# A decoder trunk on one core: other accumulator banks for a second weight tile, output stores on another queue, and accumulating loads pinned behind accumulating splits

## The chip, the core and the metric

The kernel runs on one core of a Trainium2 chip. A core has a matmul engine (TensorE, PE in the profile; its weight loads are listed apart as PEld), a vector engine (VectorE, DVE), a scalar engine (ScalarE, ACT), a general engine (GpSimd, POOL) and a synchronisation engine (SyncE, SP) that here only issues transfers. Each engine runs its own instructions in order. Transfers are issued by SyncE, ScalarE and GpSimd; the page lists their queues as q1 (SyncE's), q10 (ScalarE's) and q0 (GpSimd's). Sums of matmuls are kept in PSUM, which has eight banks here, each for 128 x 512 numbers of four bytes.

The metric is the device time of one execution in microseconds (us): a median over several runs, beside one execution that the hardware profiler recorded.

## The reference

Two layers, each of three residual blocks on x of 512 tokens by 1024 channels in float32, and a final norm:

```
for l in range(DEPTH):                                   # DEPTH = 2
    x = x + 0.5 * swiglu(rms_norm(x, ffn1_norm[l]), ffn1_wg[l], ffn1_wu[l], ffn1_wd[l])
    z = rms_norm(x, mix_norm[l]) @ w_in[l]
    attn_out = sliding_window_attention(q, k, v, attn_sink[l])   # q, k, v cut from z
    conv_out = short_conv(...)                                   # the rest of z
    x = x + concatenate([attn_out, conv_out]) @ w_out[l]
    x = x + 0.5 * swiglu(rms_norm(x, ffn2_norm[l]), ffn2_wg[l], ffn2_wu[l], ffn2_wd[l])
return rms_norm(x, final_norm)
swiglu(h, w_gate, w_up, w_down) = (silu(h @ w_gate) * (h @ w_up)) @ w_down   # 1024 -> 2816 -> 1024
```

## The kernel before

**Number format.** Every float32 operand is split into a high part "hi" of a shorter format and the rest "lo", and a product takes three matmuls: hi*hi, hi*lo and lo*hi. For weights, `split` (line 197) is a ScalarE cast (hi) and a VectorE subtraction (lo). `split_far` (line 201) spares VectorE: ScalarE writes lo = -raw, rounded to the short format (line 203), and casts hi (line 204), and then GpSimd issues a transfer that adds raw to lo (line 205); which leaves raw - hi there; the transfer waits for ScalarE.

**Weights.** A unit is one weight tile of 512 KB in one of eight "raw" buffers. `need_raw` (line 184) traces the loads up to a given unit: SyncE loads the first block of the unit (`load`, line 182), and when a unit is a sum of two blocks, GpSimd issues a second part, a transfer that adds the second block to the first (line 193). `need_split` (line 207) asks for raw units some way ahead and splits the next ones in the order of the plan; `take_split` hands the split tile to the matmuls, with splitting two tiles ahead of use.

**Stages of an FFN.** `FIRST`, `INNER` and `LAST` (lines 32 to 40) list the stages: "p" computes 256 hidden channels plainly, "w" computes 512 by a seven-product scheme (Winograd's form of Strassen) with forms a11, a12, s2, s3, s1, a22, s4, each in two halves of its contraction, "d" is the down-projection of plainly computed channels, "s" a down-projection by the seven-product scheme. INNER and LAST begin ("p", 0), ("d", (0,)), ("w", 1). In these, the weight tiles of ("d", (0,)), two of them, and form a11, half 0, of ("w", 1) are split far. The units of ("w", 1) are, in twos for the halves: a11 (one block), s1 (two blocks), a12 (one), s3 (two), a22 (one). The FFNs with INNER or LAST are the second of layer 0 and both of layer 1, so this stretch is run three times.

**Accumulators.** The eight banks have three names (`psum`, line 92): four "mm", two "sc", two "aux". `down` (line 306) goes over the eight 128-channel blocks of x. For ("d", (0,)) a weight tile covers four blocks, and the first tile is computed by `level` (lines 292 to 304), which takes its four blocks abreast in four "mm" banks; the second tile is computed by `group` (lines 265 to 286), block after block, in "mm" banks too. Behind each block VectorE adds the sum to x (line 992), and thereby frees the bank. Stage w (`winograd2`, line 863) keeps its sums "x" in "mm", "y" in "sc" and "w" in "aux". The norm's sum of squares (`factors`) uses one "aux" bank for a moment in stage p.

**Order.** The kernel's framework lays out each engine's instructions from their dependences and from the order in which the program traces them. Only the first group of the kernel and the last token tiles are ordered by hand (`manual_schedule`, for ScalarE and VectorE at the end). `tc.issue_after(ins)` makes every instruction that its block traces on the engine of `ins` follow `ins` in that engine's order, without a wait for its completion.

**The end.** `Finale.down` (line 1092) computes the last down-projection with tokens on the partitions, token tile by token tile (`piece`), and closes each tile by the norm's factor (`factor`, or `guess` and `mend`), a scaling of its two halves (`scale`, line 1111: half 0 by ScalarE at line 1118, half 1 by VectorE at line 1114), and a store of each half (line 1120): half 0 from ScalarE's queue, half 1 from SyncE's.

Of the kernel before, what the change touches and what calls it, by code (L numbers as in the profile page):

```python
# [15 lines left out]
P = 128  # L16
# [42 lines left out]
def trunk_kernel(  # L59
# [32 lines left out]
    def psum(tag, shape, name):  # L92
        return ps.tile(shape, F32, tag=tag, bufs={"mm": 4, "sc": 2, "aux": 2}[tag], name=name)
# [21 lines left out]
    def f32(ap):  # L115
        return ap.bitcast(F32)
# [67 lines left out]
    def need_raw(u):  # L184

        while state["raw"] <= min(u, len(units) - 1):
            n = state["raw"]
            _, _, kc, _, wide = units[n][0]
            r = stock(f"raw_{n}", shape=(P, kc, wide))
            if n:  # L190
                load(r, n, 0, kc)
            for more in units[n][1:]:
                nc.gpsimd.dma_start(out=r, in_=rows_of(*more), accum_op=ALU.add)  # L193
            raw_of[n] = r
            state["raw"] += 1
# [5 lines left out]
    def split_far(hi, lo, raw):  # L201

        nc.scalar.activation(lo, raw, AF.Copy, scale=-1.0)
        nc.scalar.copy(hi, raw)
        nc.gpsimd.dma_start(out=f32(lo), in_=raw, accum_op=ALU.add)

    def need_split(g):
        while state["split"] <= min(g, len(order) - 1):
            n = state["split"]
            u, what = order[n]  # L210
            far = what == "far"
            if what in (None, "wide", "far"):
                need_raw(u if far else u + LOAD_AHEAD)
                raw = raw_of.pop(u)
            elif isinstance(what, tuple):

                what, h, how = what
                far = how == "far"
                last = {"a11": 0, "a12": 4, "s2": 2, "s3": 6, "s1": 2, "a22": 8, "s4": 4}[what]
                need_raw(u + max(last, 4) + h + (0 if far else LOAD_AHEAD))  # L220
                a11, s1, a12, s3, a22 = (raw_of.get(u + 2 * i + h) for i in range(5))
                if what == "s2":
                    late = state["late"] if h else None
                    with tc.issue_after(late) if late else nullcontext():
                        nc.vector.tensor_add(a11, a11, s1)  # L225
                raw = {"a11": a11, "a12": a12, "s2": a11, "s3": s3, "s1": s1, "a22": a22, "s4": a12}[what]
            else:

                need_raw(u + 4 + LOAD_AHEAD)
                a11, a12, s1, s3, a22 = (raw_of.get(u + i) for i in range(5))  # L230
                if what == "s2":
                    nc.vector.tensor_add(a11, a11, s1)
                if what == "s4":
                    nc.vector.tensor_add(a11, a11, a12)
                raw = {"a11": a11, "a12": a12, "s2": a11, "s3": s3, "s1": s1, "a22": a22, "s4": a11}[what]
                if what == FORMS[-1]:
                    for i in range(5):
                        del raw_of[u + i]
            shape = list(raw.shape)
            hi = wpool.tile(shape, F32R, tag="wh", bufs=3, name=f"wh_{n}")  # L240
            lo = wpool.tile(shape, F32R, tag="wl", bufs=3, name=f"wl_{n}")
            if far:
                split_far(hi, lo, raw)
            elif n:
                split(hi, lo, raw)
            if isinstance(order[n][1], tuple):
                if what == "s3" and how == "share":
                    nc.gpsimd.dma_start(out=a12, in_=a11, accum_op=ALU.add)
                elif what == "s3":
                    nc.vector.tensor_add(a12, a12, a11)  # L250
                done = {"s3": (0, 3), "s1": (1,), "a22": (4,), "s4": (2,)}.get(what, ())
                for i in done:
                    del raw_of[u + 2 * i + h]
            split_of[n] = (hi, lo)
            state["split"] += 1
            if far:
                need_raw(u + LOAD_AHEAD + (4 + h if isinstance(order[n][1], tuple) else 0))

    def take_split(ahead=SPLIT_AHEAD):
        n = state["group"]  # L260
# [1 line left out]
        need_split(n + ahead if n else 0)  # L262
        return n, *split_of.pop(n)

    def group(rhs, between=None, own=None, order=range(KC)):

        n, hi, lo = own or take_split()
        acc = psum("mm", [P, S], f"acc_{n}")
        order = order[: len(rhs)]
        first, last = order[0], order[-1]  # L270
        late = n in (1, 2, 3)
        for k in order:
            if between:
                between(k, hi, lo)
            nc.tensor.matmul(acc, hi[:, k, :], rhs[k][0], start=k == first, stop=False)  # L275
            if n == 0:
                nc.tensor.matmul(acc, lo[:, k, :], rhs[k][0], start=False, stop=False)
            nc.tensor.matmul(  # L278
                acc, hi[:, k, :], rhs[k][1], start=False, stop=n == 0 and k == last
            )  # L280
            if n != 0 and not late:
                nc.tensor.matmul(acc, lo[:, k, :], rhs[k][0], start=False, stop=k == last)  # L282
        if late:
            for k in order:
                nc.tensor.matmul(acc, lo[:, k, :], rhs[k][0], start=False, stop=k == last)
        return acc
# [19 lines left out]
    def down(rhs, fresh=False):  # L306

        wide = abreast(len(rhs))
        for c in range(0, KC, wide):
            n, hi, lo = take_split()  # L310
            if fresh and c == 0:
                yield from enumerate(level(n, hi, lo, rhs, wide))
                continue
            for j in range(wide):
                cols = slice(j * P, (j + 1) * P)
                yield c + j, group(rhs, own=(f"{n}_{j}", hi[:, :, cols], lo[:, :, cols]))

    def plan():
        def cols(src, k0, kc, n, how=None):
# [683 lines left out]
    class Finale:  # L1003
# [88 lines left out]
        def down(self, rhs):  # L1092
            for half in range(2):
                gb = g2(f"gain_{half}")
                nc.sync.dma_start(
                    gb, final_norm[half * S : (half + 1) * S].partition_broadcast(P)
                )
                self.gain.append(gb)
            done = small("done", NT)
            self.widen(0, len(rhs) // 2)  # L1100
            for t in range(NT):
                rest = done[:, t : t + 1]
                acc = self.products(rhs, 0, t, 0, S)
                self.close(acc, 0, t, 0, rest)
                nc.vector.tensor_scalar(rest, rest, 1.0 / D, EPS, op0=ALU.mult, op1=ALU.add)
                if t == 0:
                    self.widen(1, len(rhs) // 2)
            def factor(t, ssq):
                return self.root(t, ssq, done[:, t : t + 1])

            def scale(t, by, h):
                y = self.y[t][h]
                if h:
                    nc.vector.scalar_tensor_tensor(
                        y, y, by, self.gain[h], op0=ALU.mult, op1=ALU.mult
                    )
                else:
                    nc.scalar.activation(y, y, AF.Copy, scale=by)
                cols = slice(h * S, (h + 1) * S)
                (nc.sync if h else nc.scalar).dma_start(out[0, t * P : (t + 1) * P, cols], y)  # L1120

            def piece(t, c0, wide):
                ssq = small(f"ssq_end{t}_{c0}", 1)
                self.close(self.products(rhs, 1, t, c0, wide), 1, t, c0, ssq)
                return ssq

            for t in range(NT - 2):
                by = factor(t, piece(t, 0, S))
                for h in (1, 0):
                    scale(t, by, h)  # L1130


            a, b = NT - 2, NT - 1
            with tc.manual_schedule(engines={act, dve}):
                ssq = piece(a, 0, S)
                early = self.guess(a, ssq, done[:, a : a + 1])
                first = piece(b, 0, H)
                by = self.mend(a, ssq, done[:, a : a + 1], early)
                scale(a, by, 0)
                second = piece(b, H, H)  # L1140
                scale(a, by, 1)
                rest = done[:, b : b + 1]
                nc.vector.scalar_tensor_tensor(
                    rest, first, 1.0 / D, rest, op0=ALU.mult, op1=ALU.add
                )
                by = self.mend(b, second, rest, self.guess(b, second, rest))
                for h in (1, 0):
                    scale(b, by, h)
# [252 lines left out]
```

## Time and profile before

| what | value |
|---|---|
| median of 3 runs | 1687.75 us (1687.32 to 1688.72) |
| the profiled execution | 1686.98 us, of which 1685.2 us are its span |
| granted clock of TensorE, mean | 0.999 |
| PE busy, share of the span | 1674.2 us, 99% |
| PEld, DVE, ACT, POOL busy | 86%, 82%, 57%, 12% |
| moved by transfers | 283.14 MB, mean 168 GB/s |

The span goes from the first to the last instruction in the profile. A row of the timeline has the start and the duration in us, the engine, the line of the program, the operation, what is written and read, and in brackets how long the engine had been idle and which instruction's end released it. Rows with a "q" behind the engine's name belong to its sequencer, which issues transfers. A row of a window has the window, its length, then busy time and number of instructions for PE, PEld, DVE, ACT and POOL, the granted clock, the busy share of the sixteen transfer engines and GB/s. A row of the list of waits has who waited for whom, the total in us, how many times, and the longest. A row of transfers has their number, their size, and the median time from issue to landing.

### The profile page before, as it was taken

How to read it: one execution, taken by the hardware profiler on the slowest of the kernel's cores; microseconds unless marked ns; L12 is line 12 of the kernel's file. 1: busy time of each engine (PE TensorE's matmuls, PEld its weight loads, DVE VectorE, ACT ScalarE, POOL GpSimd, SP SyncE). 2: the span in 40 equal slices, each digit the busy share in tenths (PEclk: the TensorE clock that was granted, in tenths of full speed). 3: DMA queues.
4: the chain of work that ended last, by engine and by line, in shares of the span. 5: the costliest groups of instructions: out<-in, count | busy, mean ns of one | idle time of the engine just before them, and what ended most of it. 6: DMA issues, size and time to landing. Idle time of an engine off the chain costs nothing.

```text
span 1685.2 us, 23535 instructions
## 1 busy us (share of the span) xinstructions
PE 1674.2 (99%) x9014; PEld 1444.2 (86%) x9014; DVE 1380.9 (82%) x1817; ACT 965.5 (57%) x1333; POOL 207.6 (12%) x186
## 2 busy tenths in 40 slices
PE   9999999999999999999999999999999999999998
PEld 7888889988898888889988888999888988888886
DVE  7987679988899967799798677997788997667995
ACT  6545565466566655564465555654565766555654
POOL 1011111001111111111011111110012111111111
PEclk9999999999999999999999999999999999999999
DMA  8467777731497677778567777875125867777881
GB/s 251 101 174 189 187 199 184 186 95 51 120 231 172 166 187 187 187 189 222 154 142 183 179 185 186 200 192 170 51 63 139 224 138 200 183 181 186 225 212 51
DMA packets 191558, 283.14 MB, mean 168 GB/s; under 512 B 8972, under 2 KB 77652, under 8 KB 191444
## 3 DMA queue, kind: packets, MB, share of 16 engines
q1 hardware_dynamic: 151108, 199.95, 37.5%
q0 software_dynamic: 39184, 80.23, 28.3%
q8 instruction: 71, 1.16, 0.3%
q10 hardware_dynamic: 1152, 1.45, 0.2%
q14 instruction: 43, 0.35, 0.1%
HBM read 261.14 MB, written 2.10 MB: 156 GB/s over the span
## 4 chain that ended last, share of the span: by engine, by line
PE 96%; DVE 3%; issue 0%; ACT 0%; ACTq 0%; DVEq 0%
PE x L713 25%; PE y L713 12%; PE x_s L698 8%; PE acc L275 8%; PE acc L278 8%; PE acc L282 7%; PE w L713 6%; PE y_s L698 4%; PE x_s L713 3%; PE w_s L698 2%; PE at L919 2%; PE x_m L698 1%; PE y_m L698 1%; PE y_s L713 1%; PE pt L1248 1%; PE x L833 1%
## 5 line engine op out<-in xcount | busy, mean ns | idle before, releaser
L198 ACT CAST wh<-raw 128x1024 fp32r<-128x1024 f32 (+1 forms) x484 | 507.3, 1048 | 545.7 <-PE x L713 131.4
L199 DVE TENSOR_TENSOR wl<-raw,wh 128x1024 fp32r<-128x1024 f32 (+1 forms) x483 | 588.9, 1221 | 209.0 <-ACT wh L198 207.4
L275 PE MATMUL acc<-xh,wh 128*128 128x512 f32 x448 | 176.4, 394 | 0.2 <-ACT xh L422 0.2
L278 PE MATMUL acc<-xl,wh 128*128 128x512 f32 x448 | 175.3, 391 | 0.1
L282 PE MATMUL acc<-xh,wl 128*128 128x512 f32 x416 | 162.3, 390 | 0.0
L193 POOL DMA_DIRECT2D raw<-in_ffn_wu_dram x39 | 47.2, 1210 | 531.6 <-DMA raw<-in_ffn_wu_dram 327.4
L278 PEld LDWEIGHTS acc<-xl,wh 128*128 128x128 f32 x448 | 84.2, 188 | 18.8 <-DVE xl L423 1.6
L275 PEld LDWEIGHTS acc<-xh,wh 128*128 128x128 f32 x448 | 84.3, 188 | 17.4 <-ACT xh L422 0.6
L282 PEld LDWEIGHTS acc<-xh,wl 128*128 128x128 f32 x416 | 78.1, 188 | 16.2
L193 POOL DMA_DIRECT2D raw<-in_ffn_wg_dram x39 | 47.2, 1233 | 228.6 <-DVE wl L199 89.6
L225 DVE TENSOR_TENSOR raw<-raw,raw 128x1024 f32<-128x1024 f32 x58 | 70.4, 1219 | 1.0 <-DMA raw<-in_ffn_wu_dram 0.4
L193 POOL DMA_DIRECT2D raw<-in_ffn_wd_dram x32 | 38.6, 1214 | 257.2 <-DMA raw<-in_ffn_wd_dram 111.5
L713 PE MATMUL w<-wh,fb21h 128*128 128x512 f32 x152 | 60.7, 399 | 0.0
L713 PE MATMUL x<-wh,ft2h 128*128 128x512 f32 x152 | 60.6, 398 | 0.0
L713 PE MATMUL y<-wh,ft3h 128*128 128x512 f32 x152 | 60.4, 398 | 0.0
L713 PE MATMUL w<-wl,fb21h 128*128 128x512 f32 x152 | 59.4, 391 | 0.0
L713 PE MATMUL x<-wl,ft2h 128*128 128x512 f32 x152 | 59.3, 390 | 0.0
L713 PE MATMUL y<-wh,ft3l 128*128 128x512 f32 x152 | 59.2, 390 | 0.0
L713 PE MATMUL y<-wl,ft3h 128*128 128x512 f32 x152 | 59.2, 390 | 0.0
L713 PE MATMUL w<-wh,fb21l 128*128 128x512 f32 x152 | 59.2, 389 | 0.0
L713 PE MATMUL x<-wl,fb11h 128*128 128x512 f32 x152 | 59.2, 389 | 0.0
L713 PE MATMUL x<-wh,fb11h 128*128 128x512 f32 x152 | 59.1, 389 | 0.0
(502 smaller groups left out, 4789.6 us busy)
## 6 DMA issues: line engine op xcount, KB each, us to landing
raw<-in_ffn_wu_dram SPq DMA_DIRECT2D x127, 512.0 KB, 3.8
raw<-in_ffn_wd_dram SPq DMA_DIRECT2D x104, 512.0 KB, 5.1
raw<-in_ffn_wg_dram SPq DMA_DIRECT2D x87, 512.0 KB, 4.8
raw<-in_ffn_wu_dram POOLq DMA_DIRECT2D x39, 512.0 KB, 8.1
raw<-in_ffn_wg_dram POOLq DMA_DIRECT2D x39, 512.0 KB, 6.0
raw<-in_w_in_dram SPq DMA_DIRECT2D x36, 512.0 KB, 3.7
raw<-in_ffn_wd_dram POOLq DMA_DIRECT2D x32, 512.0 KB, 8.0
raw<-raw POOLq DMA_DIRECT2D x20, 512.0 KB, 7.2
```

The source lines that it names most:

```text
L193: nc.gpsimd.dma_start(out=r, in_=rows_of(*more), accum_op=ALU.add)
L198: nc.scalar.copy(hi, raw)
L199: eng.tensor_sub(lo, raw, f32(hi))
L225: nc.vector.tensor_add(a11, a11, s1)
L275: nc.tensor.matmul(acc, hi[:, k, :], rhs[k][0], start=k == first, stop=False)
L278: nc.tensor.matmul(acc, hi[:, k, :], rhs[k][1], start=False, stop=n == 0 and k == last)
L282: nc.tensor.matmul(acc, lo[:, k, :], rhs[k][0], start=False, stop=k == last)
L698: nc.tensor.matmul(accs[c // 2][:, c % 2, :], w[:, k, cols], x_[:, 2 * h + k, :], start=start and c % 2 == 0 and h + k + i == 0, stop=h + ...
L713: nc.tensor.matmul(accs[u], x_[:, 2 * h + k, tok], w[:, k, :], start=start and h + k + i == 0, stop=h + k == 2 and i == 2, skip_group_chec ...
L833: nc.tensor.matmul(out, w[:, k, cols], x_[:, k, :], start=start and k + i == 0, stop=k == KC // 2 - 1 and i == 2, skip_group_check=not start,)
L919: nc.tensor.transpose(tp[:, t * P : (t + 1) * P], ups[t][:, c * P : (c + 1) * P], ident)
L1248: nc.tensor.transpose(tp[:, h, :], self.p[:, h, kb * P : (kb + 1) * P], ident)
```

## The change

Three things are changed, and nothing that is computed.

- `group` gets the name of its bank as an argument, and `down` gives the second weight tile of ("d", (0,)) the names sc, sc, aux, aux for its four blocks instead of mm.
- `split_far` returns its transfer, and the `need_raw` that follows a far split is traced under `tc.issue_after` of that transfer. Its engine is GpSimd, so this concerns the second parts (line 193). For a form that is split far, the `need_raw` ahead of the split asks only for the form's own unit; the rest is asked for behind it.
- The stores of half 0 are issued by SyncE instead of ScalarE, but for the last token tile's, which stays with ScalarE.

```diff
@@ -202,7 +202,7 @@
         nc.scalar.activation(lo, raw, AF.Copy, scale=-1.0)
         nc.scalar.copy(hi, raw)
-        nc.gpsimd.dma_start(out=f32(lo), in_=raw, accum_op=ALU.add)
+        return nc.gpsimd.dma_start(out=f32(lo), in_=raw, accum_op=ALU.add)
@@ -217,7 +217,7 @@
                 last = {"a11": 0, "a12": 4, "s2": 2, "s3": 6, "s1": 2, "a22": 8, "s4": 4}[what]
-                need_raw(u + max(last, 4) + h + (0 if far else LOAD_AHEAD))
+                need_raw(u + h if far else u + max(last, 4) + h + LOAD_AHEAD)
@@ -240,7 +240,7 @@
             if far:
-                split_far(hi, lo, raw)
+                sent = split_far(hi, lo, raw)
@@ -254,7 +254,9 @@
             if far:
-                need_raw(u + LOAD_AHEAD + (4 + h if isinstance(order[n][1], tuple) else 0))
+
+                with tc.issue_after(sent.ins):
+                    need_raw(u + LOAD_AHEAD + (4 + h if isinstance(order[n][1], tuple) else 0))
@@ -262,10 +264,10 @@
-    def group(rhs, between=None, own=None, order=range(KC)):
+    def group(rhs, between=None, own=None, order=range(KC), tag="mm"):
         n, hi, lo = own or take_split()
-        acc = psum("mm", [P, S], f"acc_{n}")
+        acc = psum(tag, [P, S], f"acc_{n}")
@@ -313,7 +315,9 @@
             for j in range(wide):
                 cols = slice(j * P, (j + 1) * P)
-                yield c + j, group(rhs, own=(f"{n}_{j}", hi[:, :, cols], lo[:, :, cols]))
+                own = (f"{n}_{j}", hi[:, :, cols], lo[:, :, cols])
+                tag = ("sc", "sc", "aux", "aux")[j] if fresh else "mm"
+                yield c + j, group(rhs, own=own, tag=tag)
@@ -1117,7 +1121,8 @@
                 cols = slice(h * S, (h + 1) * S)
-                (nc.sync if h else nc.scalar).dma_start(out[0, t * P : (t + 1) * P, cols], y)
+                queue = nc.scalar if h == 0 and t == NT - 1 else nc.sync
+                queue.dma_start(out[0, t * P : (t + 1) * P, cols], y)
```

## The prediction

> **What bounds the kernel now.** I read the page's head first, then a window over the closing stage, then the list of who waited for whom on the matmul engine.
>
> ```profile
> span 1685.2 us, 23535 instructions
> PE 1674.2 (99%) x9014; PEld 1444.2 (86%) x9014; DVE 1380.9 (82%) x1817; ACT 965.5 (57%) x1333; POOL 207.6 (12%) x186
> ```
>
> ```profile
> 1670.00:1685.20 15.20, 8.21 (x48) 7.11 (x46) 7.91 (x26) 8.22 (x19) 0.09 (x1) 0.90 0.37 141
> ```
>
> ```profile
> PE acc L275 <- DVE x L992: 1.9, 3, 0.7
> ...
> PE y_m L698 <- DVE wl L199: 0.5, 2, 0.2
> ```
>
> PE is busy 1674.2 of 1685.2 us, so 11.0 us are idle. 15.20 - 8.21 = 7.0 of them lie in the closing window, and of the other 4.0 the largest item is one kind of wait, three times, 1.9 us in all: the matmul of line 275, which writes an accumulator, waits for VectorE's eviction of line 992. Nothing in the change can be worth much more than those three waits and a part of the closing 7.0 us, unless it makes PE wait where it doesn't wait now. The three places lie in the FFNs whose stage list is not FIRST:
>
> ```profile
> 537.09 1.07 PE L301 MATMUL acc<-a,wh 128*128 128x512 f32 x4
> 538.84 0.50 PE L275 MATMUL acc<-a,wh 128*128 128x512 f32 x1 [0.68 <-DVE x L992]
> 539.40 0.40 PE L282 MATMUL acc<-a,wl 128*128 128x512 f32 x1
> ...
> 874.75 0.50 PE L275 MATMUL acc<-a,wh 128*128 128x512 f32 x1 [0.56 <-DVE x L992]
> ...
> 1371.14 0.50 PE L275 MATMUL acc<-a,wh 128*128 128x512 f32 x1 [0.68 <-DVE x L992]
> ```
>
> ```profile
> 536.96 1.23 DVE L534 TENSOR_TENSOR sums<-sums,hf 128x1024 f32<-128x1024 f32 x1
> 538.10 1.28 DVE L992 SCALAR_TENSOR_TENSOR x<-acc,x 128x512 f32<-128x512 f32 x2
> ...
> 544.50 1.88 DVE L992 SCALAR_TENSOR_TENSOR x<-acc,x 128x512 f32<-128x512 f32 x3
> ```
>
> Line 301 ends the first weight tile, whose four sums fill all four "mm" banks. Line 275 begins the second tile and needs one of them back, and VectorE comes to the first eviction only behind an operand sum (L534).
>
> **The banks.** The second tile now writes two "sc" and two "aux" banks. Nothing else uses them there: the last user of "aux" is the norm's sum of squares in the stage before, and "sc" has had none since the block before. Four matmuls of line 301 take 1.07 us and the last of them 0.39, as the row of line 282 has a usual one, so they start (1.07 - 0.39) / 3 = 0.227 us apart. A matmul that waits for nothing thus starts 0.39 - 0.227 = 0.16 us ahead of its forerunner's end, where line 275 starts 0.68 behind it: 0.84 us lost, and 0.50 - 0.39 = 0.11 more because the first matmul after the wait lasts longer, in all 0.95. The second place has 0.56 + 0.16 + 0.11 = 0.83, the third 0.95 again. Sum: 2.73 us. The other bound of this term is what the list of waits has, 1.9.
>
> Where does the lateness go? VectorE's evictions are as late as before, but the next to want banks are the two "x" sums of stage w, and these get the "mm" banks that the evictions of 538.10 free, five microseconds ahead. "aux" is wanted next by that stage's "w" sums, "sc" later still by its "y" sums (with the Finale, by transposes that wait for all eight evictions in any case).
>
> ```profile
> 550.01 5.44 PE w L713 x24
> ```
>
> The last evictions end at 544.50 + 1.88 = 546.4, and "w" will start at 550.01 - 0.95 = 549.1, so 2.7 us of cover remain. Cost: none; without that cover PE would wait for "aux" as it now does for "mm".
>
> **The second parts on POOL's queue.** This part moves work. A far split is two copies on ScalarE and an accumulating transfer that POOL issues (L205). The second part of a load whose unit is a sum of two blocks is an accumulating transfer from POOL too (L193). Before:
>
> ```profile
> 514.57 2.45 POOL L193 DMA_DIRECT2D raw<-in_ffn_wu_dram  x2 [26.68 <-DVE xl L448]
> 524.00 0.90 POOL L205 DMA_DIRECT2D wl<-raw  x1 [6.98 <-ACT wl L203]
> 529.43 0.86 POOL L205 DMA_DIRECT2D wl<-raw  x1 [4.53 <-ACT wl L203]
> 532.62 1.21 POOL L193 DMA_DIRECT2D raw<-in_ffn_wg_dram  x1 [2.32 <-DMA raw<-in_ffn_wu_dram]
> 534.12 0.90 POOL L205 DMA_DIRECT2D wl<-raw  x1 [0.29 <-DVE a L199]
> ...
> 859.97 0.90 POOL L205 DMA_DIRECT2D wl<-raw  x1 [8.51 <-ACT wl L203]
> ...
> 1356.31 0.90 POOL L205 DMA_DIRECT2D wl<-raw  x1 [6.54 <-ACT wl L203]
> ```
>
> ```profile
> 544.86 0.39 PE L713 MATMUL x<-wl,fb11h 128*128 128x512 f32 x1
> ...
> 880.78 0.39 PE L713 MATMUL x<-wl,fb11h 128*128 128x512 f32 x1
> ...
> 1377.18 0.39 PE L713 MATMUL x<-wl,fb11h 128*128 128x512 f32 x1
> ```
>
> ```profile
> 549.70 1.22 DVE L225 TENSOR_TENSOR raw<-raw,raw 128x1024 f32<-128x1024 f32 x1
> ```
>
> The order is: the two second parts of form s1 (514.57), the far transfers of down tiles 1 and 2 (524.00, 529.43), the second part of s3, half 0 (532.62), the far transfer of a11, half 0 (534.12). The pins make it: tile 1, s1 half 0, tile 2, s1 half 1, a11, then s3. So the s1 parts leave some 10 and 14 us later; they now queue behind a POOL instruction that waits for ScalarE, and who waits for them is VectorE's sum at 549.70. The a11 transfer no longer stands behind s3's part. But tile 2's and a11's transfers now each follow an s1 part closely, and a11's "wl" is read first at 544.86, 880.78 and 1377.18, which the bank part brings forward to 543.9, 879.95 and 1376.2.
>
> What does one more transfer in that line cost? From issue to landing, in windows around single rows of POOL (tile 1 at the first and the second place; the two s1 parts; s3's part; a11):
>
> ```profile
> wl<-raw POOLq DMA_DIRECT2D x1, 512.0 KB, 4.5
> ```
>
> ```profile
> wl<-raw POOLq DMA_DIRECT2D x1, 512.0 KB, 5.8
> ```
>
> ```profile
> raw<-in_ffn_wu_dram POOLq DMA_DIRECT2D x1, 512.0 KB, 5.9
> ...
> raw<-in_ffn_wu_dram POOLq DMA_DIRECT2D x1, 512.0 KB, 9.8
> ```
>
> ```profile
> raw<-in_ffn_wg_dram POOLq DMA_DIRECT2D x1, 512.0 KB, 6.0
> ...
> wl<-raw POOLq DMA_DIRECT2D x1, 512.0 KB, 7.8
> ```
>
> The two s1 parts are issued half of 2.45 us apart, so they land 9.8 + 1.2 - 5.9 = 5.1 us apart. s3's part lands at 532.62 + 6.0 = 538.6 and a11's transfer at 534.12 + 7.8 = 541.9, 3.3 us apart. A place in the line thus costs 3.3 to 5.1 us, and I take 3.3, because that pair is of the same two kinds at the same point of the stage. Tile 1 lands at 524.00 + 4.5 = 528.5, and four transfers back to back behind it bring a11 to 528.5 + 13.2 = 541.7, 2.2 us ahead of 543.9. At the second place it is 859.97 + 5.8 + 13.2 = 879.0, 1.0 ahead of 879.95; at the third (with the first's 4.5, an estimate) 1356.31 + 4.5 + 13.2 = 1374.0, 2.2 ahead of 1376.2. Tile 2 lands at 528.5 + 6.6 = 535.1, ahead of the 538.0 at which PE now wants it; the second s1 part at 538.4, well ahead of 549.70; s3's parts at 545.0 and 548.3, and their splits come behind that sum. Cost at 3.3: none. At 5.1 a11 lands at 548.9, 5.0 us late.
>
> ```profile
> q0 software_dynamic: 279, 0.57, 102.9%
> q1 hardware_dynamic: 1, 0.00, 0.2%
> ```
>
> These rows are the queues in the window 872.6 to 876. A load of SyncE's (q1) had been issued at its start, and it moved 1 packet while POOL's transfers (q0) moved 279, so I don't expect SyncE's loads to stretch POOL's line there. Here the Trainium skill speaks against the change: in "DMA: Bandwidth & Descriptors", section "Queues, rings and completion order", each DMA engine goes round-robin between the queues that have work, packet by packet. By that rule a SyncE load would share with POOL's line and stretch it toward the upper bound, the case of the first rival; this window doesn't agree with it.
>
> The a11 split now asks for no unit beyond its own before it, which puts one plain SyncE load (a12, half 0) behind it in the program. SyncE's loads keep their order among themselves, and a12 is read only by the third take of the stage, behind both halves of a11; cost none, or if it is late the same wait as a late a11.
>
> **The stores.** The closing 7.0 us hold this chain:
>
> ```profile
> 1677.92 0.72 ACT L1118 ACTIVATE ytok<-ytok,y_end 128x512 f32<-128x512 f32 x1
> 1678.67 0.34 ACTq L1120 DMA_DIRECT2D out_dram<-ytok  x1
> 1679.06 0.42 ACT L1073 ACTIVATE ysq<-ytok 128x256 f32<-128x256 f32 x1 [0.42 <-DVE ytok L1071]
> ```
>
> ```profile
> 1678.24 0.42 DVE L1071 SCALAR_TENSOR_TENSOR ytok<-end,ytok 128x256 f32<-128x256 f32 x1 [0.42 <-PE end L1064]
> ```
>
> ScalarE's last square (1679.06) has its input at 1678.24 + 0.42 = 1678.66, but the issue of token tile 2's store, 0.34 us, stands between it and the scaling. That store goes to SyncE, so the square starts at about 1678.71, and the last norm factor, scaling and stores come 0.35 us earlier. The two earlier issues on ScalarE lie ahead of waits for VectorE and are worth nothing. SyncE gets three more issues of about 0.35 us, the last ready at 1677.92 + 0.72 = 1678.64, ahead of the final stores, which stay on two queues. Bounds: 0, if SyncE's longer line delays the final store, and 1679.06 - 1678.67 = 0.39. I take 0.35, from the input's row.
>
> **Sum.** 2.73 + 0.35 = 3.08 us. The profiled execution took 1686.98 us, 1.78 us of it outside its span, and would come to 1683.90. It is 0.77 us below the median of the runs shown, 1687.75; against that median the sum gives 1684.67.
>
> **Rivals.**
>
> One, slower: a11's far transfer is late. If a place in POOL's line costs y us, PE loses 4y - 15.4, 4y - 14.2 and 4y - 15.4 at the three places, each where it is positive. The first loss comes at y = 3.55, the gain of 3.08 is used up at y = 4.0, the kernel is slower by 3.4 us at y = 4.3, and at 5.1 the places lose 5.0 + 6.2 + 5.0 = 16.2: 1684.7 + 16.2 = 1700.9. Halfway into it, at y = 4.4, they lose 2.2 + 3.4 + 2.2 = 7.8: 1692.5. For it: 5.1 stands in the trace, a stage earlier. Against: 3.3 is the row for these very transfers, and the line has holes, since tile 2's and a11's transfers wait for ScalarE.
>
> Two, the wait is not removed but moves: the instructions are laid out anew around the other banks, and PE waits for an eviction or a split a little later in the same stage. Then only the stores' 0.35 is left, 1687.4. For it: VectorE is busy nearly all the time there (L534, then L992, without a gap). Against: every bank asked for next is free microseconds ahead.
>
> Three, more comes free than I count: a new layout also removes the y_m waits (0.5 us), 1684.2. Nothing in the change touches them.
>
> **How the numbers follow.** A difference under 0.2%, 3.4 us, is about what a measurement of this kernel can't tell from none, so the line on the fast side is 1684.4. The forecast falls 0.3 us short of it, and its case is split. Forecast, with 1684.0 to 1685.7 as its own range: 0.62, of which 0.18 beyond the line. Rival one: 0.15, of which 0.10 slower by over 3.4 us. Rival two: 0.17. Rival three: 0.06, of which 0.04 beyond the line and, for a layout that turns out worse instead, 0.02 slower. Faster 0.22, within 0.66, slower 0.12. The range runs from 1683.7, rival three less the 0.4 by which the fastest run lies under the median, to 1688.6, rival two with the slowest run's 1.0 and a rival one of up to y = 4.08; about 0.15 is left out, nearly all above.
>
> **What would show it.** Right: PE waits for DVE x L992 nowhere and the first matmul of line 275's second tile lasts 0.39; POOL's rows from 524 to 536 read L205, L193, L205, L193, L205; ScalarE's last square starts 0.05 us behind VectorE's last L1071. Wrong: a wait of PE at x L713 for the DMA wl<-raw (rival one), a wait of PE for DVE x L992 at L713 or L919 (rival two), or a final store of SyncE's that starts behind ScalarE's.

## The result, and the profile after

The changed kernel takes 1683.89 us, median of 10 runs (1683.20 to 1685.67), against 1687.72 (10 runs, 1687.11 to 1691.79) of the kernel before beside it. The ratio is 0.9975, with a 95% interval of 0.9966 to 0.9985: 3.83 us or a quarter of a per cent faster. That is inside the predicted range and 0.8 us below the predicted 1684.7, but beyond the bound of 0.2%, so "within 0.2%", the likeliest outcome of the prediction, did not come true.

The profiled execution of the changed kernel took 1685.67 us, the slowest of its ten. Its head, and all rows of the list of PE's waits (who waited for whom, total us, times, longest):

```profile
span 1683.8 us, 23539 instructions
PE 1674.7 (99%) x9014; PEld 1445.5 (86%) x9014; DVE 1380.8 (82%) x1817; ACT 965.4 (57%) x1333; POOL 207.5 (12%) x186
```

```profile
PE idle L125 <- DVE warm L584: 1.2, 1, 1.2
PE xt L602 <- DMA xin<-in_x_dram: 0.7, 1, 0.7
PE y_m L702 <- DVE wl L199: 0.5, 2, 0.3
```

The three waits for VectorE's eviction are gone. The execution was slow in its opening. Matched matmul by matmul with the kernel before, it runs 1.70 us behind from there on. The second row, a late load of x, is the smaller part: the first matmul behind it is 0.57 us late. The rest arises between 7.4 and 10.5 us, where matmuls last 0.59 to 0.78 us that last 0.39 to 0.50 in the kernel before; why isn't known, and the windows' rows have a granted clock of 1.00 there. No part of the change touches the opening: just ahead of the first of the three places the banks alone and the kernel with one pin (below), which wait as long for x, lie 0.7 and 0.3 us ahead of the kernel before, and the one with the earlier update 0.2 us behind. The 1.70 has to be taken out before the traces are compared.

The three places in the timeline of PE, the last matmuls of the first weight tile and the first of the second:

```profile
538.84 1.07 PE L303 MATMUL acc<-a,wh 128*128 128x512 f32 x4
539.74 0.39 PE L277 MATMUL acc<-a,wh 128*128 128x512 f32 x1
539.97 0.39 PE L280 MATMUL acc<-a,wh 128*128 128x512 f32 x1
...
874.86 0.39 PE L277 MATMUL acc<-a,wh 128*128 128x512 f32 x1
...
1370.33 0.39 PE L277 MATMUL acc<-a,wh 128*128 128x512 f32 x1
```

Line 277 (275 before) starts 538.84 + 1.07 - 539.74 = 0.17 us ahead of the end of its forerunner and lasts 0.39, where it started 0.68 behind it and lasted 0.50. The first readers of form a11's lo tile, a few microseconds on, tell what that is worth:

```profile
545.64 0.39 PE L717 MATMUL x<-wl,fb11h 128*128 128x512 f32 x1
...
880.75 0.39 PE L717 MATMUL x<-wl,fb11h 128*128 128x512 f32 x1
...
1376.22 0.39 PE L717 MATMUL x<-wl,fb11h 128*128 128x512 f32 x1
```

Against 544.86, 880.78 and 1377.18 before, these are 0.78 late, 0.03 early and 0.96 early. From the 1.70 of the opening the three places thus gain 1.70 - 0.78 = 0.92, then 0.81, then 0.93: 2.66 us. Counted from just ahead of each place to its reader they gain 0.97, 0.86 and 0.99; a few hundredths are lost again between the places.

POOL's timeline at the first place (a row with L205 is a far transfer, one with L193 a second part):

```profile
525.75 0.86 POOL L205 DMA_DIRECT2D wl<-raw  x1 [36.17 <-ACT wl L203]
526.30 1.54 POOL L193 DMA_DIRECT2D raw<-in_ffn_wu_dram  x1
531.19 0.90 POOL L205 DMA_DIRECT2D wl<-raw  x1 [3.35 <-ACT wl L203]
531.75 1.58 POOL L193 DMA_DIRECT2D raw<-in_ffn_wu_dram  x1
535.87 0.90 POOL L205 DMA_DIRECT2D wl<-raw  x1 [2.54 <-DVE a L199]
537.13 1.21 POOL L193 DMA_DIRECT2D raw<-in_ffn_wg_dram  x1 [0.37 <-issue]
```

The order is the one that the pins write. The fifth row is a11's transfer; s3's second part, which stood ahead of it before, is now the sixth.

The closing stage, ScalarE's rows and then VectorE's:

```profile
1677.74 0.42 ACT L1077 ACTIVATE ysq<-ytok 128x256 f32<-128x256 f32 x1
...
1678.53 0.29 ACT L1083 ACTIVATE r_end<-ssq_end,done 128x1 f32<-128x1 f32 x1 [0.28 <-DVE done L1148]
1679.50 0.72 ACT L1122 ACTIVATE ytok<-ytok,y_end 128x512 f32<-128x512 f32 x1 [0.67 <-DVE y_end L406]
1680.25 0.38 ACTq L1125 DMA_DIRECT2D out_dram<-ytok  x1
```

```profile
1677.28 0.42 DVE L1075 SCALAR_TENSOR_TENSOR ytok<-end,ytok 128x256 f32<-128x256 f32 x1 [0.42 <-PE end L1068]
1677.62 0.74 DVE L1118 SCALAR_TENSOR_TENSOR ytok<-ytok,y_end,gain 128x512 f32<-128x512 f32 x1
1678.28 0.15 DVE L1148 SCALAR_TENSOR_TENSOR done<-ssq_end,done 128x1 f32<-128x1 f32 x1
```

And the end of the same chain in the kernel before:

```profile
1679.60 0.29 ACT L1079 ACTIVATE r_end<-ssq_end,done 128x1 f32<-128x1 f32 x1
1680.57 0.72 ACT L1118 ACTIVATE ytok<-ytok,y_end 128x512 f32<-128x512 f32 x1 [0.67 <-DVE y_end L402]
1681.32 0.35 ACTq L1120 DMA_DIRECT2D out_dram<-ytok  x1
```

The last square starts 1677.74 - 1677.28 = 0.46 us behind the start of VectorE's last line 1075, where it was 0.82: the 0.36 that was forecast. But the norm's factor behind it (r_end) now starts 0.79 behind the square, where it was 1679.60 - 1679.06 = 0.54, because it waits for VectorE's update of `done`, which stands behind a scaling of 0.74 us. So only 0.11 of the 0.36 is left there. From the issue of the last store to the span's end it is 1683.8 - 1680.25 = 3.55 us, where it was 1685.2 - 1681.32 = 3.88, another 0.33. The stage ends 0.11 + 0.33 = 0.44 us earlier in all. The second part isn't scatter: in the eight profiled kernels with the stores' edit (those below included) the last store, ScalarE's, takes 2.6 us from issue to landing, in the six profiles without it 2.9.

Opening aside, the two profiles thus differ by 2.66 and 0.44: 3.1 us, what the prediction summed up. The medians differ by 3.83. The other 0.7 us is what the experiments had to find.

### The profile page after: what moved, and what is told of

It is laid out like the page before. It is cut to its first block, busy times and chain, and to the rows that moved or that the text cites. A ratio compares the mean times of both kernels' runs of the same rounds, so it can differ in the third digit from the quotient of the medians.

```text
span 1683.8 us, 23539 instructions
## 1 busy us (share of the span) xinstructions
PE 1674.7 (99%) x9014; PEld 1445.5 (86%) x9014; DVE 1380.8 (82%) x1817; ACT 965.4 (57%) x1333; POOL 207.5 (12%) x186
## 4 chain that ended last, share of the span: by engine, by line
PE 97%; DVE 2%; DMA 0%; issue 0%; ACT 0%; SPq 0%; DVEq 0%; ACTq 0%
PE x L717 25%; PE y L717 12%; PE x_s L702 8%; PE acc L277 8%; PE acc L280 8%; PE acc L284 7%; PE w L717 6%; PE y_s L702 4%; PE x_s L717 3%; PE w_s L702 2%; PE at L923 2%; PE x_m L702 1%; PE y_m L702 1%; PE y_s L717 1%; PE pt L1253 1%; PE x L837 1%
## 5 line engine op out<-in xcount | busy, mean ns | idle before, releaser
L193 POOL DMA_DIRECT2D raw<-in_ffn_wu_dram x39 | 48.9, 1257 | 405.7 <-DMA raw<-in_ffn_wu_dram 207.0
L193 POOL DMA_DIRECT2D raw<-in_ffn_wg_dram x39 | 47.2, 1229 | 226.3 <-DMA raw<-in_ffn_wu_dram 144.4
L193 POOL DMA_DIRECT2D raw<-in_ffn_wd_dram x32 | 38.6, 1205 | 258.4 <-DMA raw<-in_ffn_wd_dram 176.0
L717 PE MATMUL x<-wl,ft1h 128*128 128x512 f32 x152 | 59.2, 389 | 0.0
```

The costliest lines, as they stand in the source:

```text
L717: nc.tensor.matmul(accs[u], x_[:, 2 * h + k, tok], w[:, k, :], start=start and h + k + i == 0, stop=h + k == 2 and i == 2, skip_group_chec ...
```

## The experiments

"Place" is one of the three stretches, "a11" the far transfer of form a11's half 0. The kernel before, run beside the first four kernels below, took 1687.74; beside the fifth to the eighth 1687.54; beside the ninth 1687.58.

### The banks alone

The kernel before with only this:

```diff
-    def group(rhs, between=None, own=None, order=range(KC)):
+    def group(rhs, between=None, own=None, order=range(KC), tag="mm"):
...
-        acc = psum("mm", [P, S], f"acc_{n}")
+        acc = psum(tag, [P, S], f"acc_{n}")
...
-                yield c + j, group(rhs, own=(f"{n}_{j}", hi[:, :, cols], lo[:, :, cols]))
+                own = (f"{n}_{j}", hi[:, :, cols], lo[:, :, cols])
+                tag = ("sc", "sc", "aux", "aux")[j] if fresh else "mm"
+                yield c + j, group(rhs, own=own, tag=tag)
```

> Only the banks of the second tile are changed. Theory (the banks do nearly all of it): no wait of PE for DVE x L992 is left, PE gains 0.90, 0.80 and 0.92 us at the three places as in the changed kernel's profile, 2.6 in all, and the time is 1685.1 (1687.7 less 2.6). Rival (the pins are what lets the banks pay): in the old order of POOL a11's transfer lands only 0.2 us ahead of the new need at the second place, so PE waits there for wl at line L713 or L717, and 0.3 to 0.8 of the gain is lost. Second rival (a part of the change is worth 0.7 us more than its rows show): the time is below 1684.6.

Measured: 1685.94 (11 runs, 1683.87 to 1689.41), ratio 0.9989 (0.9980 to 0.9997). The waits for VectorE are gone and each place gains what it gains in the full change. But one row in the list of PE's waits is new against the profile of before:

```profile
PE x L715 <- DMA wl<-raw: 1.2, 1, 1.2
```

At the second place PE waits for a11. So 1.80 us of the banks' 2.66 show in the median, and the kernel scatters over 5.5 us.

### The pins alone

The kernel before with the edits in `split_far` and `need_split`, but neither other banks nor stores:

```diff
-                need_raw(u + max(last, 4) + h + (0 if far else LOAD_AHEAD))
+                need_raw(u + h if far else u + max(last, 4) + h + LOAD_AHEAD)
...
-                need_raw(u + LOAD_AHEAD + (4 + h if isinstance(order[n][1], tuple) else 0))
+                with tc.issue_after(sent.ins):
+                    need_raw(u + LOAD_AHEAD + (4 + h if isinstance(order[n][1], tuple) else 0))
```

> Only the order of POOL's second parts is changed. Theory: it costs and gains nothing, 1687.7, with PE's three waits for DVE x L992 as before (0.95, 0.83, 0.95 us lost) and a11 landing 1.0 to 2.0 us ahead of its reader. Rival (the order itself frees something, the missing 0.7 us): 1687.0 or less. Rival on the other side (the longer line makes a11 late): a wait of PE for DMA wl<-raw, up to 2 us in all, 1689.7.

Measured: 1687.08 (11 runs, 1686.68 to 1687.30), ratio 0.9997 (0.9988 to 1.0006). The profiled execution (1686.94) matches that of before (1686.98) nearly matmul by matmul, with the same three waits of 1.9 us. Yet the median is 0.66 us below that of before, and the runs lie within 0.62 us of each other, where those of before beside them spread over 3.0. The interval of the ratio can't tell it from 1; what the 0.66 is, the last experiment shows.

### The stores alone

```diff
-                (nc.sync if h else nc.scalar).dma_start(out[0, t * P : (t + 1) * P, cols], y)
+                queue = nc.scalar if h == 0 and t == NT - 1 else nc.sync
+                queue.dma_start(out[0, t * P : (t + 1) * P, cols], y)
```

> Only the stores are changed. Theory: 0.15 us in the closing chain, since the last norm factor now waits for VectorE's update of 'done' instead of ScalarE's store, and 0.3 between the last store's issue and the end: 1687.2. Rival (the 0.3 behind the last issue is scatter of one execution): 1687.5. Second rival (the stores hold the missing 0.7): 1686.5 or less.

Measured: 1687.13 (11 runs, 1686.43 to 1688.39), ratio 0.9997 (0.9989 to 1.0006); in the profile the closing stage ends 0.44 us earlier. The factor waits for `done` as it does in the full change. The profiled execution took 1688.00 all the same: it has a wait of 1.1 us for a11 at the second place, which nothing in this edit touches, and which the first profile of before doesn't have.

### The full change without the pins

Banks and stores, no pins.

> The changed kernel without the pins: banks and stores. Theory: the same as the changed kernel, 1683.9 to 1684.6, and no wait of PE for wl. Rival (the pins are needed): slower than the changed kernel by 0.3 to 0.8 us, with a wait of PE for wl at the second place.

Measured: 1685.21 (11 runs, 1683.81 to 1685.56), ratio 0.9983 (0.9974 to 0.9992), again with a wait of 1.2 us for a11 at the second place. The full change lies 1685.21 - 1683.89 = 1.3 us lower. So the pins are worth more with the new banks, whose reader of a11 comes earlier. But a late a11 costs 1.5 us by matched matmuls here, no more than with the old banks; what differs seems to be how often it is late, since eight of the eleven runs lie above 1685.0 and only two below 1684.1. Why it is late more often isn't shown.

### a11 forced to the end of POOL's line

The changed kernel, with s3's load and second part traced ahead of a11's split and the split's transfer pinned behind that part:

```diff
-                nc.gpsimd.dma_start(out=r, in_=rows_of(*more), accum_op=ALU.add)
+                state["more"] = nc.gpsimd.dma_start(out=r, in_=rows_of(*more), accum_op=ALU.add)
...
-            if far:
+            if far and isinstance(order[n][1], tuple):
+                need_raw(u + 6)
+                with tc.issue_after(state["more"].ins):
+                    sent = split_far(hi, lo, raw)
+            elif far:
                 sent = split_far(hi, lo, raw)
```

> The changed kernel, but a11's far transfer is put behind the second part of s3, half 0, so that it again queues behind a part that waits for SyncE's load, with the two s1 parts in the line as well. Theory (what the pins buy is that a11's transfer doesn't stand behind s3's part): with 3.2 to 3.6 us for one more place, a11 lands about 2 us behind its reader at each of the three places, PE waits 1.5 to 2.7 us three times for wl, and the time is 1688.5 to 1692. Rival (the pins pay through the s1 parts or by a quieter schedule, and a11's place in the line doesn't matter): 1683.9, no wait for wl.

Measured: 1695.02 (5 runs, 1691.38 to 1698.92), ratio 1.0047 (1.0034 to 1.0060). PE now waits for a11 at all three places:

```profile
PE x L721 <- DMA wl<-raw: 7.0, 3, 3.6
```

That is rival one's mechanism at work, and it comes from s3's part ahead of a11. The price is higher than it was expected to be: three waits of 7.0 us in all, but some 11 us lost. PE's timeline at the second wait, and two windows behind it:

```profile
884.30 0.50 PE L721 MATMUL x<-wl,fb11h 128*128 128x512 f32 x1 [3.58 <-DMA wl<-raw]
...
886.04 0.63 PE L721 MATMUL x<-wl,fb11h 128*128 128x512 f32 x1
886.47 0.63 PE L721 MATMUL x<-wh,fb11h 128*128 128x512 f32 x1
```

```profile
886.00:889.00 3.00, 3.00 (x9) 2.33 (x8) 0.32 (x1) 1.04 (x1) 0.00 (x0) 0.52 0.58 106
889.00:892.00 3.00, 3.00 (x15) 2.47 (x14) 3.00 (x3) 1.18 (x2) 0.00 (x0) 1.00 0.00 0
```

From 886 to 889 the granted clock is 0.52, and matmuls start 0.43 us apart instead of 0.227: another 1.6 us, off the trace by pairing matmuls. The third wait is followed by the same, the first isn't. With some 0.3 us more at each place, the lost head start and the longer matmul behind a wait, this makes up the 11 us.

### Only a11's pin

The changed kernel, but only the loads behind a11's far transfer are pinned; those behind the far transfers of the two down tiles go where they went before:

```diff
-                with tc.issue_after(sent.ins):
+                pinned = isinstance(order[n][1], tuple)
+                with tc.issue_after(sent.ins) if pinned else nullcontext():
```

> The changed kernel with only the pin behind a11's transfer; the two s1 parts go out early as before the change. Theory (the one pin is the useful one): 1683.9, as tight as the changed kernel, no wait of PE for wl, and a11 lands 3 us or more ahead of its reader instead of 1.0 to 1.5. Rival (the late s1 parts are what keeps SyncE's load and tile 2's transfer apart): PE waits about 1.2 us for wl at the second place in some executions, median 1684.5 to 1685.3.

Measured: 1683.82 (11 runs, 1683.53 to 1683.85), ratio 0.9978 (0.9969 to 0.9987); the full change has 1683.89. No wait for a11. POOL's rows and PE's reader at the second place:

```profile
869.66 0.86 POOL L205 DMA_DIRECT2D wl<-raw  x1 [4.57 <-DVE sums L538]
871.57 1.21 POOL L193 DMA_DIRECT2D raw<-in_ffn_wg_dram  x1 [1.06 <-DMA raw<-in_ffn_wu_dram]
```

```profile
878.69 0.39 PE L718 MATMUL x<-wl,fb11h 128*128 128x512 f32 x1
```

a11 (L205) leaves without waiting for the load ahead of s3's part (L193); it takes 6.8 us and lands at 876.4, 2.3 us ahead of its reader (4.2 at the two other places; 3 or more was expected at each). In the full change it lands later against its reader:

```profile
871.75 0.90 POOL L205 DMA_DIRECT2D wl<-raw  x1 [3.31 <-DVE sums L537]
```

```profile
wl<-raw POOLq DMA_DIRECT2D x1, 512.0 KB, 7.6
```

That is 871.75 + 7.6 = 879.3, 1.4 us ahead of 880.75. So of the moves that the pins make, only s3's part behind a11 is worth something; the two s1 parts between the far transfers use up margin and give nothing.

### One other bank instead of four

```diff
-                tag = ("sc", "sc", "aux", "aux")[j] if fresh else "mm"
+                tag = ("sc", "mm", "mm", "mm")[j] if fresh else "mm"
```

> The changed kernel with only the first block of the second tile in an sc bank and the other three in mm. Theory (only the first eviction of each place was late; each later block needs its bank 2.7 us after the one before and VectorE clears one in 0.6 to 1.9): the same as the changed kernel, 1683.9, no wait for DVE x. Rival (the later blocks would wait too once the first doesn't): 0.3 to 1 us lost at each place, 1685 to 1687.

Measured: 1684.59 (11 runs, 1683.89 to 1684.71), ratio 0.9982 (0.9973 to 0.9991), 0.7 us above the full change. The second tile itself no longer waits, but the stage behind it does. PE and VectorE at the first place:

```profile
544.80 0.94 PE L717 MATMUL x<-wh,fb11h 128*128 128x512 f32 x2
545.58 0.39 PE L717 MATMUL x<-wh,fb11l 128*128 128x512 f32 x1
```

```profile
544.50 1.88 DVE L996 SCALAR_TENSOR_TENSOR x<-acc,x 128x512 f32<-128x512 f32 x3
```

From 544.80 two matmuls and the next should start 0.227 apart; the third starts at 545.58 instead of 545.25, so the second, which starts late and lasts longer, lost 0.33 us. It opens stage w's second "x" sum and takes an "mm" bank that VectorE is only now evicting. The same costs some 0.3 at the third place, and nothing at the second. The theory that one bank does it all fell: the other three spare the sums of the next stage.

### The update of `done` moved ahead

The changed kernel, with these lines of the hand-written order moved up:

```diff
                 scale(a, by, 0)
+                rest = done[:, b : b + 1]
+                nc.vector.scalar_tensor_tensor(
+                    rest, first, 1.0 / D, rest, op0=ALU.mult, op1=ALU.add
+                )
                 second = piece(b, H, H)
                 scale(a, by, 1)
-                rest = done[:, b : b + 1]
-                nc.vector.scalar_tensor_tensor(
-                    rest, first, 1.0 / D, rest, op0=ALU.mult, op1=ALU.add
-                )
```

> The changed kernel, with VectorE's update of 'done' for the last token tile put ahead of the second half's closing instead of behind the scaling of the tile before. Theory (with the store gone from ScalarE's order, the last norm factor waits for this update, 0.28 us idle in the changed kernel's row): the factor starts 0.23 us earlier and the time is 1683.65. Rival (the chain is bound by ScalarE's square anyway): no change in the row, 1683.9.

Measured: 1683.45 (10 runs, 1683.18 to 1683.90), ratio 0.9973 (0.9964 to 0.9982). VectorE's update, and ScalarE's last square and factor:

```profile
1675.30 0.16 DVE L1146 SCALAR_TENSOR_TENSOR done<-ssq_end,done 128x1 f32<-128x1 f32 x1
```

```profile
1676.19 0.42 ACT L1077 ACTIVATE ysq<-ytok 128x256 f32<-128x256 f32 x1
...
1676.74 0.30 ACT L1083 ACTIVATE r_end<-ssq_end,done 128x1 f32<-128x1 f32 x1
```

The factor is back at 0.55 behind the square (0.79 in the full change), and the closing stage ends 0.26 us earlier. So the 0.36 of the square reaches the stores whole once this second wait is out of the way too.

### Only a11's pin, and the update moved ahead

The last edit and that of "Only a11's pin" together.

> The changed kernel with both finds together: only the pin behind a11's transfer, and the early update of 'done'. Theory (they lie in different stages and add up): 1683.82 of the one pin less the 0.24 between square and factor, 1683.5 to 1683.6, no wait of PE for wl. Rival (the lower median of the early update came from the opening's scatter): 1683.8.

Measured: 1683.60 (10 runs, 1683.47 to 1683.86), ratio 0.9976 (0.9966 to 0.9985), 0.3 us under the full change's 1683.89. From the one before it, 1683.45, it can't be told apart. Both medians lie below the changed kernel's, and both profiles show the earlier factor; but the intervals of the ratios overlap, and the kernel before itself measured 0.2 us apart beside these kernels.

### The kernel before, three times more

Nothing is changed; three more profiles, to see whether the wait for a11 at the second place comes and goes.

> The kernel before, unchanged, profiled once more, for the 0.7 us that three partial changes showed. Theory (the second place's a11 transfer is late in most executions of the kernel before, and the first profile caught one where it isn't): a wait of PE for DMA wl<-raw at L713 near 881 us, about 1.2 us, and a time above 1687.6. Rival (only the partial kernels have that wait): no such wait.

> The kernel before, unchanged, a third profile. Theory (the wait for wl at the second place comes in about half of its executions): either a wait of PE for DMA wl<-raw at L713 near 881 us with a time near 1688, or no such wait and a time near 1687.0. Rival (the scatter of the kernel before has another seat): a time above 1687.5 without that wait.

> The kernel before, unchanged, a fourth profile. Theory and rival as for the third: the time is above 1687.5 if, and only if, PE waits for DMA wl<-raw near 881 us.

Measured: 1686.95, 1688.16 and 1688.52 us. With the first profile (1686.98) there are four executions. Those of 1686.95 and 1686.98 don't wait for a11; the two others wait 1.1 and 1.2 us at the second place. POOL's rows there, first in the first profile of before, then in the last:

```profile
870.64 1.21 POOL L193 DMA_DIRECT2D raw<-in_ffn_wg_dram  x1 [4.33 <-DMA raw<-in_ffn_wu_dram]
871.36 1.42 POOL L205 DMA_DIRECT2D wl<-raw  x1
```

```profile
872.68 1.21 POOL L193 DMA_DIRECT2D raw<-in_ffn_wg_dram  x1 [6.48 <-DMA raw<-in_ffn_wu_dram]
873.40 1.42 POOL L205 DMA_DIRECT2D wl<-raw  x1
```

```profile
882.11 0.50 PE L713 MATMUL x<-wl,fb11h 128*128 128x512 f32 x1 [1.23 <-DMA wl<-raw]
```

s3's second part (L193) waits for SyncE's load of its first part, 4.33 us in the one and 6.48 in the other, and a11's transfer (L205), next in POOL's order, stands behind it. It leaves at 873.40 instead of 871.36, lands 8.7 us later at 882.1, and PE starts then. The load is issued when a raw buffer comes free, while the second down tile's far transfer is under way too. Both, from issue to landing, in the first profile and in the last:

```profile
wl<-raw POOLq DMA_DIRECT2D x1, 512.0 KB, 7.1
raw<-in_ffn_wu_dram SPq DMA_DIRECT2D x1, 512.0 KB, 4.3
```

```profile
wl<-raw POOLq DMA_DIRECT2D x1, 512.0 KB, 5.6
raw<-in_ffn_wu_dram SPq DMA_DIRECT2D x1, 512.0 KB, 5.9
```

In these two, where the one is quicker, the other is slower, as if they raced; so it is in the profiles of the banks alone, the stores alone and the change without the pins, all with the late a11 (load 5.8 to 5.9, far transfer 5.5 to 5.7). In the profile of 1688.16 the load took 5.5 although the far transfer had 7.1, so the race isn't all of it, and what delays the load there stays open. A late a11 loses 1.4 to 1.6 us, the lost head start and the slower matmul behind the wait included, and two profiles of four have it, so some 0.7 us on average. That answers to the 0.66 of the pins alone and to the 0.77 by which the first profile lay under its median. The share rests on four profiles alone; the kernels with a11 ahead of s3's part bear it out by their narrow runs, 0.62 us with the pins alone and 0.32 with one pin and the other banks.

## Why the prediction was right or wrong

**The banks: right.** Forecast 2.73 from 0.95, 0.83 and 0.95; measured 0.92, 0.81 and 0.93, 2.66 net, or 0.97, 0.86 and 0.99 at the places themselves. The other bound, the 1.9 of the list of waits, leaves out that the next matmul could have started ahead of its forerunner's end and lasts longer behind a wait. That the lateness would vanish in the sums of stage w was right, and the kernel with one other bank shows what pays for it: without the four names those sums wait some 0.3 us at two places.

**The stores: right in size, by another way.** Forecast 0.35; the closing stage gains 0.44 with the stores alone and in the full change. The square comes 0.36 earlier as said. But I took the square as the only thing that the factor waits for, and didn't look at VectorE's line: its update of `done`, behind a scaling, ended last once the square was early. That the size came out was luck: 0.33 behind the issue of the last store, which the prediction didn't have, made up for it. Why the last store lands sooner wasn't tried and stays open.

**The pins: the step that failed.** It is the end of "The second parts on POOL's queue": "Cost: none", where the whole part was priced as a risk and never as a gain. That a11's transfer no longer stands behind s3's part was seen and put at nothing, without a reason; in the one profiled execution it came 1.0 us in time at the second place. In two of four profiles it does not, and s3's place ahead of it costs PE 1.4 to 1.6 us there: 0.66 us in the median with the old banks, 1.3 with the new ones, where more of the runs seem to have it. The hint was on the page: the profiled execution lay 0.77 us below the median of its own kernel, which the prediction noted and carried along as an offset. With 2.66 of the banks, 0.44 of the stores and 0.66 of the pins the sum is 3.76, and 1687.72 - 3.76 = 1683.96 against the measured 1683.89.

**The price of a place in POOL's line: right.** Forecast 3.3 us, with 5.1 as the other bound. From tile 1's landing to a11's, over four, it came out at 3.6, 3.2 and 3.6 us in the profile after, and a11 landed 1.2, 1.4 and 1.0 us ahead of its reader. The holes that spoke against the first rival weren't there: at all three places each transfer of the line was issued before the one ahead of it had landed. In the Trainium skill ("DMA: Bandwidth & Descriptors", "Queues, rings and completion order") each DMA engine goes round-robin between the queues that have work; by that rule SyncE's loads were to share with POOL's line and stretch it toward the upper bound. It wasn't stretched that far, though the load's 4.3 and 5.9 us beside the second tile's far transfer of 7.1 and 5.6 suggest that the two queues do take from each other.

**The rivals.** One (a11 late) is a real mechanism, but the change takes it away rather than bringing it: it shows in two profiles of the kernel before and in those of the banks alone, the stores alone and the change without the pins, and it takes 11 us in the kernel that forces it. Two (the wait moves) didn't happen with four names. Three's waits for y_m are still there, 0.5 us. Of what would show the forecast right, all came: the last square starts 0.04 us behind the end of line 1075 (1677.28 + 0.42 = 1677.70), the order on POOL is as given, no matmul waits for an eviction at the three places, and line 275's first matmul (277 now) lasts 0.39; only the time lies lower, by the pins' part.

**The chances.** The 0.2% line was 0.3 us below the forecast, and 0.22 was given to what lay beyond it. A gain for the pins of even half a microsecond would have moved the forecast over it.

## What to carry to other kernels

When the profiled execution lies apart from the median of its own kernel by more than other runs scatter, find out which wait it lacks before pricing a change: take a second profile, and compare the list of waits. An engine that issues transfers in order passes on the wait of each to all behind it, so a transfer that somebody will read soon shouldn't stand behind one that waits for a load from another queue, even where the trace at hand shows it in time by a microsecond. And when a chain is shortened, look at every input of its next step, since the second latest is the new end.

## What was unexpected of the hardware

Short stalls of TensorE can cost more than their length. In the kernel that forces a11 late, the waits of 3.58 and 1.81 us were followed by 3 to 4 us at a granted clock of 0.52 and 0.60 and so cost about 1.6 us more each, while behind the wait of 1.58 us it stayed at 1.00, and behind the waits of 1.1 and 1.2 us at the second place of before only some 0.1 to 0.2 was lost on top. The profile's rows for the third place:

```profile
1383.52 0.55 PE L721 MATMUL x<-wl,fb11h 128*128 128x512 f32 x1 [1.81 <-DMA wl<-raw]
```

```profile
1383.00:1387.00 4.00, 3.48 (x9) 2.75 (x10) 2.18 (x3) 0.00 (x0) 1.20 (x1) 0.60 0.13 28
```

Whether it goes by length, with a step between 1.58 and 1.81 us, or by something else, three waits can't tell.

And a transfer's time varies between executions of one program where two queues want the transfer engines at once: the same load of 512 KB took 4.3 us in the first profile of the kernel before and 5.5 and 5.9 in the two late ones, and with it the whole kernel took 1.2 to 1.6 us longer.
